# Rotary part once per group of three token tiles, and the work of GpSimd on data in both projections moved to VectorE

## The chip, the cores and the metric

The kernel runs on one core of a Trainium2 chip. The metric is the device time of one execution in microseconds (us); the median of three runs of the kernel before is 2882.1 us (2879.1 to 2884.48). A core has five engines with an instruction queue each: TensorE (PE in the rows, with its weight loads as PEld), VectorE (DVE), ScalarE (ACT), GpSimd (POOL) and SyncE (SP), which issues the DMAs. An engine works its queue in order; a semaphore holds an instruction until what it reads is there.

## The reference

Two layers, each with one input projection of 128 context tokens and 2048 latent tokens (17 tiles of 128), four mixers side by side, an output projection, a residual and a layer norm:

```python
h = x * (1 + scale) + shift
u = h @ p['w_in'] + p['b_in']
...
gq = rms_norm(gq.reshape(B, L, GQA_HEADS, HEAD_DIM), p['q_norm'])     # 4 heads of 64
gk = rms_norm(gk.reshape(B, L, GQA_KV_HEADS, HEAD_DIM), p['k_norm'])  # 2 heads of 64
...
g_out = blocked_attention(axial_rope(gq), ...axial_rope(gk)...)
c_out = conv_mix(c_v, c_glu, ...)   # val * sigmoid(glu), 31 taps along the tokens, LayerNorm, silu, 256x256 product
...
x = layer_norm(DEEPNORM_ALPHA * x + gate * out, p['ln_g'], p['ln_b'])
```

`rms_norm(x, g)` is x / sqrt(mean(x*x) + eps) * g; `axial_rope` turns pairs of a head's columns by angles that depend on the token's place in a 64-wide grid. Context tokens get no rotation. Everything is float32.

## The kernel before

**Precision.** Each factor of a large product is split into a high part (a copy on ScalarE to the engine's reduced float format) and a low part (value minus high part, one subtract). The product is three matmuls: high by high, low by high, high by low (lines 300 to 302). So every operand costs a copy on ScalarE and a subtract; before, most of the subtracts run on GpSimd: `hlo` of the activations (L385, the odd pieces; the even ones on VectorE), `wlo` of the weights (L419), `evl` (L597), `ql` and `ks` of the rotated queries and keys (L722, L732), the convolution's and the pool's operands (L824, L891) and `mlo` of the output projection (L1493).

**Stages.** In each layer phase 1 is the input projection (`_phase1`), phase 2 the grouped-query attention, phase 3 the neighbourhood attention, phase 4 the output projection (`_phase4`). In the profiled execution phase 1 runs from 0 to 727 us in the first layer and from 1490 to 2142 in the second, phase 4 from 1228 to 1490 and from 2640 to 2875.

**Phase 1.** The tokens are taken in two halves, and in each half the column blocks of the projection in a fixed order: three blocks of the convolution, then `gkv` (keys and values), `gq` (queries), and others. `gkv` and `gq` are worked by token tiles: 24 matmuls of 128x256 a tile, into one of five PSUM buffers named `ps_u`. VectorE takes a tile out of PSUM (`qb`, L657, and for values `gve`, L660). So the tile five further on can't begin before that is done.

**What a tile of `gkv` and `gq` sets off.** ScalarE squares it, VectorE sums the squares (L671). For three tiles together the reciprocal root `rs` is made; then for each tile VectorE multiplies by `rs` (L691), GpSimd by the norm's weight (L696), VectorE makes the rotation of the tile in four instructions (L713 to L716), ScalarE makes the high part and GpSimd the low one (`ks` L731 and L732, `qd` and `ql` L720 and L722), and TensorE transposes the tile (L738) between the matmuls of a later tile. Which steps come after how many tiles is given by a list, `later.add(n, step)`.

**Lanes.** After every unit of 24 matmuls a `tick` runs due steps and lets other work on: lane A is the 31-tap convolution of the half on VectorE, one instruction a tap and channel block (L769, 128x1166, or 128x1040 in the second half), one a tick in `gkv` and `gq`. The order in each engine's queue is then settled by the framework's scheduler, from its own estimate of the times.

**Phase 4.** For each token tile the mixers' output `mx` is split (`mhi` L1489 on ScalarE, `mlo` L1493 on GpSimd), multiplied, and VectorE makes the residual and the layer norm in instructions of 128x1024 (L1508, L1515, L1516, L1539, L1540), whose result `y` TensorE transposes (L1557). 

Of the kernel before, what the change touches and what calls it, by code (L numbers as in the profile page):

```python
# [122 lines left out]
class Kern:  # L123
# [248 lines left out]
    def prep_hk(self, l, c, k, x, hi, lo, start=False):  # L372
# [30 lines left out]
    def prep_w(self, l, b, half):  # L403
# [10 lines left out]
        for q in range(4):  # L414
# [4 lines left out]
            nc.gpsimd.tensor_tensor(lo[:, ks, :], w, f32(hi[:, ks, :]), op=ALU.subtract)  # L419
# [15 lines left out]
    def _phase1(self, l):  # L435
# [26 lines left out]
        def tick(ins):  # L462
# [93 lines left out]
    def evac_ch(self, l, name, m, g0, n, p):  # L556
# [26 lines left out]
        else:  # L583
# [13 lines left out]
            nc.gpsimd.tensor_tensor(el[:, :n], e[:, :n], f32(eh[:, :n]), op=ALU.subtract)  # L597
# [81 lines left out]
    def rms(self, l, name, t0, nt, nh, qb, rs):  # L679
# [6 lines left out]

        def s1():
# [6 lines left out]
            g = self.qkn[:, 0 if name == "gq" else 1, :]  # L694
# [7 lines left out]
        def s2(t):  # L702
            tg = t0 + t
            if tg:
                t1 = self.rp.tile([128, 256], F32, tag="t1", name="t1")
                t2 = self.rp.tile([128, 256], F32, tag="t2", name="t2")
                v1 = t1[:, :w].rearrange("p (h d) -> p h d", d=64)
                v2 = t2[:, :w].rearrange("p (h e d) -> p h e d", e=2, d=32)
                qv = q4[:, t]
                qs = qb[:, t, :w].rearrange("p (h e d) -> p h e d", e=2, d=32)  # L710
                cb = rp[:, t, 0, :].unsqueeze(1).to_broadcast([128, nh, 64])
# [32 lines left out]
        for t in range(nt):  # L744
            self.later.add(1 + (t + 1) // 2, lambda t=t: s2(t))
# [981 lines left out]
```

## Time and profile before

| | |
|---|---|
| median of three runs | 2882.1 us |
| profiled execution, device time | 2877.41 us |
| its span, first to last instruction | 2875.5 us |
| mean granted TensorE clock, share of full speed | 0.986 |
| TensorE, VectorE, ScalarE, GpSimd busy | 96%, 68%, 38%, 38% |

The shares are means over stages with different limits: TensorE is the busy one nearly everywhere, so what counts is where it stood still, where it ran at a lower granted clock, and what it waited for then. An engine that is busy less than TensorE can still be full in a short stretch.

### The profile page before, as it was taken

The numbers are of one execution on the slowest core, as the hardware profiler recorded it, in microseconds if no ns is written. First come the engines' busy times: TensorE is split into PE (matmuls) and PEld (weight loads), VectorE is DVE, ScalarE is ACT, GpSimd is POOL, SyncE is SP. The second block draws the span as 40 slices with busy tenths as digits, with TensorE's granted clock in tenths as the row PEclk, the third lists the DMA queues.
The fourth block names the chain that finished last, engine by engine and source line by source line (L and its number), as shares of the span: only waits on it lengthen the run. The fifth ranks groups of instructions, "written<-read, shape, count | busy, mean of one in ns | idle before, by whom it ended". The sixth has DMA issues, their size and how long they took to land. (4 is left out here: it accounts for less than half of the span.)

```text
span 2875.5 us, 45443 instructions
## 1 busy us (share of the span) xinstructions
PE 2773.3 (96%) x16960; PEld 2265.7 (79%) x16960; DVE 1963.2 (68%) x3503; ACT 1080.6 (38%) x1922; POOL 1093.0 (38%) x716
## 2 busy tenths in 40 slices
PE   8999999999999999999999999999999999999998
PEld 6989989999555556887889899999985555578887
DVE  2895247944488886749868952398437888677587
ACT  4233431333344445542222344313424444465210
POOL 4353320411466666014322533213225666720232
PEclk9999999999899999999999999999999999999999
DMA  8676675655451005647755556746555201076343
GB/s 324 206 214 202 196 248 184 211 185 152 96 140 35 21 21 155 166 139 242 234 182 182 171 184 176 239 146 222 154 151 129 67 21 35 8 204 184 132 168 103
DMA packets 330876, 447.79 MB, mean 156 GB/s; under 512 B 54176, under 2 KB 266656, under 8 KB 327840
## 3 DMA queue, kind: packets, MB, share of 16 engines
q1 hardware_dynamic: 330656, 444.89, 51.0%
q8 instruction: 134, 2.20, 0.3%
q14 instruction: 86, 0.70, 0.1%
HBM read 279.39 MB, written 165.39 MB: 155 GB/s over the span
## 5 line engine op out<-in xcount | busy, mean ns | idle before, releaser
L300 PE MATMUL ps_u<-hhi,whi 128*128 128x384 f32 (+1 forms) x1712 | 564.8, 333 | 10.3 <-ACT hhi L383 5.6
L301 PE MATMUL ps_u<-hlo,whi 128*128 128x384 f32 (+1 forms) x1712 | 564.4, 330 | 0.9 <-DVE hlo L385 0.7
L302 PE MATMUL ps_u<-hhi,wlo 128*128 128x384 f32 (+1 forms) x1712 | 562.9, 329 | 0.5 <-POOL wlo L419 0.4
L1053 POOL TENSOR_TENSOR zp<-zp,e 128x1024 f32<-128x1024 f32 x160 | 386.7, 2417 | 217.5 <-ACT e L1035 213.9
L1035 ACT ACTIVATE e<-ps_d 128x1024 f32<-128x1024 f32 x288 | 292.5, 1026 | 361.8 <-PE ps_d L1033 328.9
L769 DVE SCALAR_TENSOR_TENSOR cacc<-cz,small,cacc 128x1166 f32<-128x1166 f32 (+1 forms) x240 | 355.8, 1483 | 3.5
L300 PEld LDWEIGHTS ps_u<-hhi,whi 128*128 128x128 f32 x1712 | 324.0, 190 | 19.5 <-ACT hhi L383 9.4
L301 PEld LDWEIGHTS ps_u<-hlo,whi 128*128 128x128 f32 x1712 | 324.2, 189 | 5.3 <-issue 1.7
L302 PEld LDWEIGHTS ps_u<-hhi,wlo 128*128 128x128 f32 x1712 | 324.0, 189 | 3.2 <-POOL wlo L419 1.4
L956 DVE TENSOR_REDUCE mx<-ps_s 128x1 f32<-128x512 f32 (+1 forms) x374 | 228.5, 631 | 123.3 <-PE ps_s L953 119.3
L1041 PE MATMUL ps_a<-e,gvv 128*64 128x512 f32 x1152 | 280.9, 609 | 0.0
L1493 POOL TENSOR_TENSOR mlo<-mx,mhi 128x512 fp32r<-128x512 f32 x66 | 109.7, 1683 | 407.1 <-ACT mhi L1489 322.6
L300 PE MATMUL ps_u<-whi,hhi 128*128 128x256 f32 x816 | 236.3, 290 | 0.0
L302 PE MATMUL ps_u<-whi,hlo 128*128 128x256 f32 x816 | 235.1, 288 | 0.0
L301 PE MATMUL ps_u<-wlo,hhi 128*128 128x256 f32 x816 | 235.1, 288 | 0.0
L419 POOL TENSOR_TENSOR wlo<-ws,whi 128x512 fp32r<-128x512 f32 x92 | 136.2, 1490 | 211.3 <-ACT whi L418 195.1
L1522 PE MATMUL ps_d<-woh,mhi 128*128 128x512 f32 x512 | 200.3, 391 | 0.0
L1523 PE MATMUL ps_d<-wol,mhi 128*128 128x512 f32 x512 | 200.2, 391 | 0.0
L1524 PE MATMUL ps_d<-woh,mlo 128*128 128x512 f32 x512 | 199.6, 390 | 0.0
L1015 PE MATMUL ps_d<-q,k 128*128 128x512 f32 x576 | 187.9, 409 | 2.3 <-ACT e L1035 1.7
L1033 PE MATMUL ps_d<-q,k 65*128 65x512 f32 x560 | 178.3, 400 | 0.0
L1041 PEld LDWEIGHTS ps_a<-e,gvv 128*64 128x64 f32 x1152 | 71.7, 137 | 127.5 <-issue 125.1
(285 smaller groups left out, 5488.2 us busy)
## 6 DMA issues: line engine op xcount, KB each, us to landing
ws<-in_w_in SPq DMA_DIRECT2D x96, 256.0 KB
mw<-in_w_mod SPq DMA_DIRECT2D x32, 512.0 KB
nq<-s_nq SPq DMA_DIRECT2D x64, 256.0 KB
mx<-s_mix SPq DMA_DIRECT2D x16, 1024.0 KB
s_gate<-ev SPq DMA_DIRECT2D x80, 192.0 KB
s_qh<-qT SPq DMA_DIRECT2D x34, 256.0 KB
x<-in_x SPq DMA_DIRECT2D x17, 512.0 KB
s_xT<-xo SPq DMA_DIRECT2D x17, 512.0 KB
```

The source lines that it names most:

```text
L300: mm(p, ah, bh, start=(k == 0), stop=False)
L301: mm(p, ah, bl, start=False, stop=False)
L302: return mm(p, al, bh, start=False, stop=(k == 7))
L769: nc.vector.scalar_tensor_tensor(acc[:, c, :n], z[:, k:k + n], cw[:, c, k:k + 1], acc[:, c, :n], op0=ALU.mult, op1=ALU.add)
L956: r = nc.vector.tensor_reduce(mx[:, h, i:i + 1], p[:, :n], axis=AX.X, op=ALU.max)
L1015: nc.tensor.matmul(s[:, kv * 512:(kv + 1) * 512], k1[kv][:, j * 128:(j + 1) * 128], q1[:, 2 * kv:2 * kv + 2, :].rearrange("p h t -> p (h t ...
L1035: nc.scalar.activation(e, s, AF.Exp)
L1041: nc.tensor.matmul(acc[kv * 64:(kv + 1) * 64, :], vv[:, j, kv * 64:(kv + 1) * 64], e[:, kv * 512:(kv + 1) * 512], start=(j == 0), stop=(j ...
L1053: nc.gpsimd.tensor_tensor(zp, zp, e, op=ALU.add)
L1522: nc.tensor.matmul(o, hi[:, k, :], woh[:, k, ns], start=(k == 0), stop=False)
L1523: nc.tensor.matmul(o, hi[:, k, :], wol[:, k, ns], start=False, stop=False)
L1524: nc.tensor.matmul(o, lo[:, k, :], woh[:, k, ns], start=False, stop=(k == 7))
```

## The change

Four things. (1) The rotation works on a group of three tiles: the norm's weight is multiplied into the table of cosines and sines (`rp`), once a group, and then five instructions do what 12 on VectorE and three on GpSimd did, beside one multiply by `rs` where there were three. The context tile gets a table row made of the weight and of zero, by GpSimd. (2) The subtracts named above are given to VectorE. (3) `h` (L382, before on VectorE outside the start) is made by ScalarE. (4) The tap lane does no tap or one, alternately, in a tick of `gq`, and the step `s2` of the group's tile t stands t+1 ticks behind, in place of 1+(t+1)//2. The lines of the kernel after are a few lower: L653 is the old L657, L667 the old L671, L694 the old L691, L703 and L706 the old L713 to L716, L727 the old L732, L733 the old L738, L764 the old L769, L415 the old L419.

```diff
-            if start:
-                nc.scalar.activation(h[:, a:b], x[:, a:b], AF.Identity, bias=sh, scale=sc)
-            else:
-                nc.vector.tensor_scalar(h[:, a:b], x[:, a:b], sc, sh, op0=ALU.mult, op1=ALU.add)
+            nc.scalar.activation(h[:, a:b], x[:, a:b], AF.Identity, bias=sh, scale=sc)
...
-        eng = nc.gpsimd if k % 2 or start else nc.vector
-        eng.tensor_tensor(lo[:, k, :n], h[:, :n], f32(hi[:, k, :n]), op=ALU.subtract)
+        nc.vector.tensor_tensor(lo[:, k, :n], h[:, :n], f32(hi[:, k, :n]), op=ALU.subtract)
...
-            nc.gpsimd.tensor_tensor(lo[:, ks, :], w, f32(hi[:, ks, :]), op=ALU.subtract)
+            nc.vector.tensor_tensor(lo[:, ks, :], w, f32(hi[:, ks, :]), op=ALU.subtract)
...
-                for _ in range(1 if name in ("gkv", "gq") else 2):
+                for _ in range({"gkv": 1, "gq": 1 - odd}.get(name, 2)):
...
+        tab = rp[:, l0 - t0:nt].rearrange("p t c d -> p (t c) d")
+        nc.vector.tensor_tensor(tab, tab, g.unsqueeze(1).to_broadcast([128, k, 64]), op=ALU.mult)
+        if t0 == 0:
+            nc.gpsimd.memset(rp[:, 0, 1, :], 0.0)
+            nc.gpsimd.tensor_copy(rp[:, 0, 0, :], g)
...
-            for t in range(nt):
-                nc.vector.tensor_tensor(
-                    q4[:, t], q4[:, t], rs[:, t, :nh].unsqueeze(2).to_broadcast([128, nh, 64]), op=ALU.mult
-                )
-            for t in range(nt):
-                nc.gpsimd.tensor_tensor(
-                    q4[:, t], q4[:, t], g.unsqueeze(1).to_broadcast([128, nh, 64]), op=ALU.mult
-                )
+            nc.vector.tensor_tensor(
+                q4, q4, rs[:, :nt, :nh].unsqueeze(3).to_broadcast([128, nt, nh, 64]), op=ALU.mult
+            )
...
+            for i in range(2):
+                cb = rp[:, :nt, i, :].unsqueeze(2).to_broadcast([128, nt, nh, 64])
+                nc.vector.tensor_tensor(v[i], q4, cb, op=ALU.mult)
+            for f in range(2):
+                nc.vector.tensor_tensor(o[:, :, :, f, :], a[:, :, :, f, :], b[:, :, :, 1 - f, :], op=ALU.add)
...
-                nc.vector.tensor_tensor(v1, qv, cb, op=ALU.mult)
-                nc.vector.tensor_tensor(v2[:, :, :, 0:16], qs[:, :, :, 16:32], sb[:, :, :, 0:16], op=ALU.mult)
-                nc.vector.tensor_tensor(v2[:, :, :, 16:32], qs[:, :, :, 0:16], sb[:, :, :, 16:32], op=ALU.mult)
-                nc.vector.tensor_tensor(qb[:, t, :w], t1[:, :w], t2[:, :w], op=ALU.add)
...
-                nc.gpsimd.tensor_tensor(ql, q4[:, t], f32(qd[:, :, 0, :]), op=ALU.subtract)
+                nc.vector.tensor_tensor(ql, q4[:, t], f32(qd[:, :, 0, :]), op=ALU.subtract)
...
-                nc.gpsimd.tensor_tensor(ks[:, :, 1, :], q4[:, t], f32(ks[:, :, 0, :]), op=ALU.subtract)
+                nc.vector.tensor_tensor(ks[:, :, 1, :], q4[:, t], f32(ks[:, :, 0, :]), op=ALU.subtract)
...
-            self.later.add(1 + (t + 1) // 2, lambda t=t: s2(t))
+            self.later.add(1 + t, lambda t=t: s2(t))
```

The same swap of `nc.gpsimd` for `nc.vector` stands at L597, L824, L891 and L1493. GpSimd's queue goes from 721 instructions to 253, VectorE's from 3505 to 3639, ScalarE's from 1780 to 1876; TensorE's and SyncE's keep theirs. The scheduler then orders the queues anew.

TensorE in the second layer, the first place where a transpose of keys stands among the matmuls of a `gkv` tile (`ps_u`: the tile's PSUM buffer, `ps_d`: the transpose's, `idr`: the identity). Before, it is in the sixth tile of the block:

```order
L301 MATMUL ps_u_15794<-wlo_15423,hhi_14793 128x256
L302 MATMUL ps_u_15794<-whi_15422,hlo_14794 128x256
L300 MATMUL ps_u_15794<-whi_15422,hhi_14793 128x256
L738 MATMUL ps_d_15786<-idr_63,ks_15676 128x128 x2
L301 MATMUL ps_u_15794<-wlo_15423,hhi_14793 128x256
L302 MATMUL ps_u_15794<-whi_15422,hlo_14794 128x256
L300 MATMUL ps_u_15858<-whi_15422,hhi_14959 128x256
```

After, the first two stand together in the ninth tile:

```order
L302 MATMUL ps_u_15768<-whi_15262,hlo_14800 128x256
L300 MATMUL ps_u_15768<-whi_15262,hhi_14799 128x256
L301 MATMUL ps_u_15768<-wlo_15263,hhi_14799 128x256
L733 MATMUL ps_d_15618<-idr_63,ks_15520 128x128 x2
L733 MATMUL ps_d_15660<-idr_63,ks_15579 128x128 x2
L302 MATMUL ps_u_15768<-whi_15262,hlo_14800 128x256
L300 MATMUL ps_u_15768<-whi_15262,hhi_14799 128x256
```

The transposes moved back by three tiles, while the matmuls around them are the same.

VectorE in the same layer, in the block of queries of the first half (`cacc` is a tap of the convolution, `t` the products of the rotation, `rp` its table). Before, the rotation goes tile by tile, between taps:

```order
L713 TENSOR_TENSOR t_16339<-qb,rp 128x256
L714 TENSOR_TENSOR t_16340<-qb,rp 128x8x16
L715 TENSOR_TENSOR t_16340<-qb,rp 128x8x16
L769 SCALAR_TENSOR_TENSOR cacc<-cz,small,cacc 128x1166
L713 TENSOR_TENSOR t_16381<-qb,rp 128x256
L714 TENSOR_TENSOR t_16382<-qb,rp 128x8x16
L715 TENSOR_TENSOR t_16382<-qb,rp 128x8x16
L716 TENSOR_TENSOR qb<-t_16339,t_16340 128x256
L657 TENSOR_TENSOR qb<-ps_u,btok 128x256 x3
L769 SCALAR_TENSOR_TENSOR cacc<-cz,small,cacc 128x1166
```

After, a group of three tiles goes through in a few wider instructions, and the low parts of weights and keys stand between them:

```order
L706 TENSOR_TENSOR qb<-t_15812,t_15813 128x3x4x16 x2
L694 TENSOR_TENSOR qb<-qb,rs 128x768
L764 SCALAR_TENSOR_TENSOR cacc<-cz,small,cacc 128x1166
L686 TENSOR_TENSOR rp<-rp,qkn 128x384
L727 TENSOR_TENSOR ks<-qb,ks 128x2x64 x2
L703 TENSOR_TENSOR t_15945<-qb,rp 128x768
L703 TENSOR_TENSOR t_15946<-qb,rp 128x768
L764 SCALAR_TENSOR_TENSOR cacc<-cz,small,cacc 128x1166
L727 TENSOR_TENSOR ks<-qb,ks 128x2x64
L706 TENSOR_TENSOR qb<-t_15945,t_15946 128x24x16 x2
L764 SCALAR_TENSOR_TENSOR cacc<-cz,small,cacc 128x1166
L653 TENSOR_TENSOR qb<-ps_u,btok 128x256 x3
```

Where three instructions for a tile and one tap alternated, two wide products and two wide sums now stand, with `L727`, which was GpSimd's, between them.

## Rows read from the trace of the kernel before

**Rows 1.** The page's first part: busy time, share of the span, instructions.

```profile
PE 2773.3 (96%) x16960; PEld 2265.7 (79%) x16960; DVE 1963.2 (68%) x3503; ACT 1080.6 (38%) x1922; POOL 1093.0 (38%) x716
```

**Rows 2.** TensorE's waits: us in total, times, longest us.

```profile
PE ps_d L738 <- POOL ks L732: 12.0, 8, 3.5
PE ps_d L738 <- ACT qd L720: 9.0, 7, 3.2
...
PE ps_s L1557 <- DVE y L1540: 3.7, 5, 1.9
...
PE ps_d L795 <- DVE cacc L769: 2.4, 1, 2.4
```

**Rows 3.** Busy time by stretch; last columns: clock, DMA share, GB/s.

```profile
132.00:172.00 40.00, 34.71 (x281) 32.53 (x282) 36.49 (x84) 12.28 (x39) 19.05 (x25) 0.87 0.59 182
205.00:212.00 7.00, 5.97 (x36) 5.06 (x35) 7.00 (x16) 2.71 (x5) 3.10 (x3) 1.00 0.70 217
1576.00:1608.00 32.00, 26.29 (x192) 25.55 (x192) 30.80 (x65) 9.11 (x25) 17.48 (x19) 0.89 0.58 177
1636.00:1672.00 36.00, 29.09 (x167) 27.93 (x166) 35.66 (x60) 14.74 (x29) 20.26 (x19) 0.95 0.66 210
```

**Rows 4.** TensorE's timeline at such a wait, start and duration in us.

```profile
131.21 0.28 PE L300 MATMUL ps_u<-whi,hhi 128*128 128x256 f32 x1
134.75 0.50 PE L738 MATMUL ps_d<-idr,ks 128*128 128x128 f32 x2 [3.26 <-POOL ks L732]
```

**Rows 5.** The same view by stretch, second layer, convolution to the queries' end.

```profile
1562.00:1642.00 80.00, 71.62 (x535) 69.89 (x534) 77.64 (x135) 23.89 (x58) 40.96 (x38) 0.96 0.56 175
sum 122.00, PE 113.62 PEld 111.89 DVE 118.78 ACT 34.27 POOL 50.11; mean PE 56.81 PEld 55.94 DVE 59.39 ACT 17.14 POOL 25.05
```

**Rows 6.** VectorE's costliest lines from 1520 to 1642 us.

```profile
L769 DVE SCALAR_TENSOR_TENSOR cacc<-cz,small,cacc 128x1166 f32<-128x1166 f32 x49 | 80.6, 1646 | 0.9
L691 DVE TENSOR_TENSOR qb<-qb,rs 128x128 f32<-128x128 f32 (+1 forms) x15 | 7.0, 519 | 0.0
L715 DVE TENSOR_TENSOR t<-qb,rp 128x64 f32<-128x64 f32 (+1 forms) x12 | 6.1, 512 | 0.0
...
L713 DVE TENSOR_TENSOR t<-qb,rp 128x128 f32<-128x128 f32 (+1 forms) x12 | 5.5, 459 | 0.8 <-POOL qb L696 0.6
...
L716 DVE TENSOR_TENSOR qb<-t,t 128x128 f32<-128x128 f32 (+1 forms) x11 | 3.6, 335 | 0.0
```

**Rows 7.** VectorE's timeline in the second layer's queries.

```profile
1636.09 0.94 DVE L713 TENSOR_TENSOR t<-qb,rp 128x256 f32<-128x256 f32 x1 [0.63 <-POOL qb L696]
...
1638.44 2.46 DVE L769 SCALAR_TENSOR_TENSOR cacc<-cz,small,cacc 128x1166 f32<-128x1166 f32 x1
1640.83 0.41 DVE L713 TENSOR_TENSOR t<-qb,rp 128x256 f32<-128x256 f32 x1
...
1641.90 1.07 DVE L657 TENSOR_TENSOR qb<-ps_u,btok 128x256 f32<-128x256 f32 x3
```

**Rows 8.** GpSimd's timeline in the same stretch.

```profile
1634.18 3.45 POOL L696 TENSOR_TENSOR qb<-qb,qkn 128x256 f32<-128x256 f32 x3
...
1638.33 1.34 POOL L419 TENSOR_TENSOR wlo<-ws,whi 128x512 fp32r<-128x512 f32 x1
```

**Rows 9.** VectorE's timeline in the first layer, a tap at its shortest.

```profile
119.90 1.42 DVE L769 SCALAR_TENSOR_TENSOR cacc<-cz,small,cacc 128x1166 f32<-128x1166 f32 x1
121.24 0.27 DVE L671 TENSOR_REDUCE rs<-sq 128x2 f32<-128x128 f32 x1
```

**Rows 10.** All of line 1493: duration in ns, least, median, most.

```profile
L1493 POOL TENSOR_TENSOR mlo<-mx,mhi x66: 1267/1313/2357, 1231.2 to 2847.1; 128x512 fp32r<-128x512 f32 x66
...
L1493 DVE TENSOR_TENSOR mlo<-mx,mhi x2: 691/692/693, 1229.8 to 2641.4; 128x512 fp32r<-128x512 f32 x2
```

**Rows 11.** Who waited for line 382: us in total, times.

```profile
  ACT hhi L383: 86.1, 53
```

**Rows 12.** Busy time in phase 4 of the first layer.

```profile
1300.00:1368.00 68.00, 64.70 (x312) 53.20 (x311) 63.29 (x77) 20.84 (x43) 30.40 (x20) 1.00 0.75 244
```

More of the change, by code (lines that the diff above doesn't have):

```diff
@@ L596, in evac_ch @@
             el = self.e2.tile([128, 384], F32R, tag="evl", name="evl")
-            nc.gpsimd.tensor_tensor(el[:, :n], e[:, :n], f32(eh[:, :n]), op=ALU.subtract)
+            nc.vector.tensor_tensor(el[:, :n], e[:, :n], f32(eh[:, :n]), op=ALU.subtract)
             for hh in range(2):
@@ L685, in rms @@
         nc.sync.dma_start(rp[:, l0 - t0:nt], A["rope"][:, l0 - 1:t0 + nt - 1])
+        g = self.qkn[:, 0 if name == "gq" else 1, :]
+        k = 2 * (t0 + nt - l0)
+        tab = rp[:, l0 - t0:nt].rearrange("p t c d -> p (t c) d")
[3 more added lines that the diff above has]
+            nc.gpsimd.tensor_copy(rp[:, 0, 0, :], g)
         def s1():
@@ L689, in s1 @@
             nc.vector.reciprocal(rs[:, :nt, :nh], rs[:, :nt, :nh])
-            for t in range(nt):
-                nc.vector.tensor_tensor(
-                    q4[:, t], q4[:, t], rs[:, t, :nh].unsqueeze(2).to_broadcast([128, nh, 64]), op=ALU.mult
-                )
-            g = self.qkn[:, 0 if name == "gq" else 1, :]
-            for t in range(nt):
-                nc.gpsimd.tensor_tensor(
-                    q4[:, t], q4[:, t], g.unsqueeze(1).to_broadcast([128, nh, 64]), op=ALU.mult
-                )
+            nc.vector.tensor_tensor(
+                q4, q4, rs[:, :nt, :nh].unsqueeze(3).to_broadcast([128, nt, nh, 64]), op=ALU.mult
+            )
+            t1 = self.rp.tile([128, 3, 256], F32, tag="t1", name="t1", bufs=1)
+            t2 = self.rp.tile([128, 3, 256], F32, tag="t2", name="t2", bufs=1)
+            v = [x[:, :nt, :w].rearrange("p t (h d) -> p t h d", d=64) for x in (t1, t2)]
+            for i in range(2):
+                cb = rp[:, :nt, i, :].unsqueeze(2).to_broadcast([128, nt, nh, 64])
+                nc.vector.tensor_tensor(v[i], q4, cb, op=ALU.mult)
+            o, a, b = [x[:, :nt, :w].rearrange("p t (h f d) -> p t h f d", f=2, d=16) for x in (qb, t1, t2)]
+            for f in range(2):
+                nc.vector.tensor_tensor(o[:, :, :, f, :], a[:, :, :, f, :], b[:, :, :, 1 - f, :], op=ALU.add)
             if t0 == 0 and name == "gkv":
@@ L823, in conv_post @@
             nc.scalar.activation(shi[:, c, :n], s32[:, :n], AF.Copy)
-            nc.gpsimd.tensor_tensor(slo[:, c, :n], s32[:, :n], f32(shi[:, c, :n]), op=ALU.subtract)
+            nc.vector.tensor_tensor(slo[:, c, :n], s32[:, :n], f32(shi[:, c, :n]), op=ALU.subtract)
             yield
@@ L890, in pool_jobs @@
             nc.scalar.activation(yhi[:, :n], y, AF.Copy)
-            nc.gpsimd.tensor_tensor(ylo[:, :n], y, f32(yhi[:, :n]), op=ALU.subtract)
+            nc.vector.tensor_tensor(ylo[:, :n], y, f32(yhi[:, :n]), op=ALU.subtract)
             if i + 1 < len(items):
@@ L1491, in prep @@
                     self.midact = getattr(r, "ins", r)
-                eng = nc.vector if t == 0 and k.start == 0 else nc.gpsimd
-                eng.tensor_tensor(lo[:, k], m[:, k, ms], f32(hi[:, k]), op=ALU.subtract)
+                nc.vector.tensor_tensor(lo[:, k], m[:, k, ms], f32(hi[:, k]), op=ALU.subtract)
             hl[t] = (hi, lo)
@@ L1658, in layouts @@
         rope[:, 0, o + 16:o + 32] = co
-        rope[:, 1, o:o + 16] = -si
-        rope[:, 1, o + 16:o + 32] = si
+        rope[:, 1, o:o + 16] = si
+        rope[:, 1, o + 16:o + 32] = -si
     m["rope"] = c(rope.reshape(L // 128, 128, 2, 64).transpose(1, 0, 2, 3))
```

9 lines of the change are left out of this document (removed).

## The prediction, made before the changed kernel was run

> **What bounds the kernel now.** I read the busy shares of the page first, then TensorE's waits, then the busy time of every engine by stretch, and last the two queues that release the waits, line by line and in order of time.
>
> TensorE is busy 2773.3 of the 2875.5 us of the span [rows 1], so 102 us of idle time, and what a lower granted clock costs on top, are all that a change which leaves the matmuls alone can win. The list of waits shows the largest group: the transposes of rotated keys and queries, L738, waited 12.0 us in 8 cases for the low part of keys on GpSimd and 9.0 us in 8 cases for the high part of queries on ScalarE [rows 2]. A longest case shows how it looks: the matmul at 131.21 is followed by nothing until 134.75, a wait of 3.26 us [rows 4]. The instruction waiting is small, but it stands in the queue among the matmuls of a later tile, so all of TensorE waits.
>
> The view by stretch says what this costs in all [rows 3]. The four stretches are the blocks of keys and queries of the first half of the tokens, two in each layer. In their 115.0 us TensorE is busy 96.06 by the four rows together, so 18.94 us are idle. The granted clock is 0.87, 0.89 and 0.95 in three of them, against 1.00 in the fourth: 0.13 x 40 + 0.11 x 32 + 0.05 x 36 = 10.5 us more. Together 29.5 us stand to be had. In the same stretches VectorE is busy 109.95 us, 96%. So the engine that ends these waits is VectorE, though the list names GpSimd and ScalarE: both work on what VectorE hands them, and they are far from full there.
>
> **Why VectorE is full there, and what the change makes of it.** From 1520 to 1642 us, the convolution's last block up to the sixteenth tile of the second layer, VectorE is busy 118.78 of 122 us [rows 5]. 49 taps take 80.6 us of it, 1.646 each, and the multiply by the root and the rotation take 62 instructions of 28.3 us (7.0 + 6.1, and L714 the same 6.1, + 5.5 + 3.6) [rows 6]. But a tap takes 1.42 us at its shortest, and the next instruction starts 1.34 after it: an instruction is covered by its successor for 0.08 us [rows 9]. What stretches them stands beside them in time: at 1636.09 the product of the rotation takes 0.94 us while GpSimd does three multiplies by the weight, and at 1640.83 the same takes 0.41 with GpSimd's queue empty; the tap at 1638.44 takes 2.46 beside a weight subtract of GpSimd [rows 7, 8].
>
> The rule behind it is in the Trainium skill, "SBUF — State Buffer", section "Who interferes with whom": the two engines share a port pair, and a VectorE instruction that needs it and a GpSimd one lock each other out. The rows agree in direction; the tap lost 1.04 us, less than the 1.34 of the GpSimd instruction beside it, so a plain sum of lock times would overstate the gain.
>
> I now count VectorE's queue up to the evacuation of the sixteenth tile in the order after, and price each instruction start to start, its shortest duration less 0.08:
>
> - 46 taps (three fewer, by the lane that skips every other tick of the queries) at 1.34: 61.6.
> - 14 weight subtracts of 128x512 that were GpSimd's, at the 0.69 that VectorE took for this shape in the output projection [rows 10], less 0.08: 8.5.
> - 9 `ks` of 128x128 at 0.27 [rows 9] and 3 `ql` of 128x256 at 0.41 [rows 7]: 2.7.
> - Rotation and root, 25 instructions in place of 62. The shapes are wider than any of before: 0.41 for 256 columns and 0.69 for 512 give 0.28 for 256 more, so 0.55 for 384, 0.97 for 768, 0.34 for 192. Four table products at 0.55, 3 x 0.55 + 2 x 0.97 for the root, 6 x 0.55 + 2 x 0.97 for the products, 6 x 0.34 + 2 x 0.55 for the sums are 14.2, less 25 x 0.08: 12.2. If a strided sum costs by columns as the uncontended tap does (1.42 for 1166), nothing changes; if each cost as in the stretched rows it would be some 20.
> - The other 49 instructions: before they took 118.8 - (80.6 - 3.9) - (28.3 - 5.0) = 18.8 us; at the least 49 x 0.20 [rows 9] = 9.8. I take 14.
>
> The sum is 99 us against 118.8, with the last item's ends 95 to 104. So VectorE comes to the sixteenth tile about 17 us sooner (some of its 3 us of idle stay), at 1625 and not 1642. TensorE lost 8.4 us idle and 0.04 x 80 = 3.2 by the clock from 1562 to 1642 [rows 5], and without these it would come to the same point at 1630. VectorE is then 5 us ahead of TensorE where it was behind.
>
> In the first layer the count gives 40 taps, 16 weight subtracts and the same rotation, and only some 6 us are won, while TensorE has 10.5 us to win from 132 to 172 [rows 3]; so there I keep part of the loss.
>
> **The sum.** Against the profiled execution, 2877.4 us (span 2875.5):
>
> - The waits of the transposes and their clock: -29.5.
> - Waits that stay or are new: +10. In the order after, a transpose of keys stands three tiles later, which at 24 matmuls of 0.12 us (131.21 is one of a row of such) is some 8 us more room against a longest wait of 3.5 [rows 2]. But a tile's keys now come only after the whole group of three. I keep 5 us for the PSUM buffers in the first layer, by the 4.5 us that VectorE stays behind there, and 5 us for 4 of the 16 waits at their mean of 1.3. The ends are 0 and the whole 21.
> - The clock in two of these: +3.5 (the stretch from 1636 on lost 1.8 with one wait of that size [rows 3]); ends 0 and 10.5.
> - The wait of L795 for the last tap [rows 2]: -2.4. With the taps shorter it goes; at worst it stays.
> - Output projection: `mlo` and the weights go to VectorE, which was busy 63.29 of 68 us in its fullest part [rows 12]. `mlo` costs 0.69 there against a median of 1.31 on GpSimd [rows 10]. The 66 `mlo` lie in some 500 us of the two output projections, so 9 in those 68 us, 6.2 us more on VectorE, where 4.7 are free; but the pieces of `h` for the next layer leave it, and what runs beside GpSimd, which the queries' rows show up to twice as long, gets shorter (GpSimd is busy 30.40 us there). I take these as even, so the wait of L1557 for `y`, 3.7 us, mostly goes: -2.5 (ends -3.7 and +4, if VectorE fills up and nothing gets shorter).
> - `h` on ScalarE, 96 instructions: ScalarE had already waited 86.1 us for `h` in its queue [rows 11], and is busy 12.28 of 40 us in the full stretch [rows 3], so this is hidden, except at the start and where a half begins, where nothing else is ready: +1.5 (0 to 8, for 8 pieces of 0.5 at two places).
> - The rest that leaves GpSimd (`evl`, the convolution's and pool's operands) lies beside matmuls and has slack: 0 (-2 to 2). TensorE's and SyncE's instructions keep their number.
>
> -29.5 + 10 + 3.5 - 2.4 - 2.5 + 1.5 = -19.4, so 2858.0 in the state of the profile. That execution was 4.7 us below the median of the three runs, 2882.1; so the forecast there is 2862.7, rounded 2863.
>
> **Rivals.**
>
> *The waits only move.* The late step isn't VectorE's load but the round trip VectorE, ScalarE, VectorE, TensorE. A step of a group of three comes later for its first tile, and a `ks` in VectorE's queue stands behind taps of 1.4 us each, up to two. For it: the list names ScalarE in 8 of the 16 waits [rows 2]. Against: VectorE's 96% and the later place of the transposes. Then 29.5 us are lost as before in another line, and the time is that of before, 2878 to 2886.
>
> *VectorE becomes the bound.* If the stretch of the taps is not GpSimd's doing (DMAs run at 0.56 to 0.70 share too [rows 3, 5]), 46 taps stay at 1.57 start to start, 72 us; the weight subtracts then cost up to what GpSimd's took, 1.34 less 0.08, 14 x 1.26 = 17.6; with 2.7, 12.2 and 18.8 the sum is 123.3, 4.5 more than before. TensorE is then held at the PSUM buffers, from the twenty-first tile on, in place of the transposes: 4.5 us in each layer, half as much again by the clock (10.5 to 18.94 in rows 3), 13.5 in all, and 1.5 at the start; won are only the two small terms, 2.4 and 2.5: 2882.1 + 15 - 4.9 = 2892. It decides from taps of 1.6 us mean on. Against it: 0.41 and 0.94 us for the same instruction [rows 7].
>
> The Trainium skill's "Perfetto Trace Analysis", section "Optimizing Scalar/DVE Operations", says that when VectorE is saturated, offloading some of its work to another engine may make sense, and adds that between VectorE and GpSimd it might not help, for the shared port. Its first half speaks for this rival, its second against; the rows with 0.94 and 0.41 bear out the second.
>
> *A larger gain.* All 21 us of L738 with their clock go and the start costs nothing: 2882.1 - 29.5 - 4.9 = 2848.
>
> **How the numbers follow.** Forecast 0.60, larger gain 0.06, waits only move 0.18, VectorE the bound 0.16. About 0.2% (5.8 us) is what a measurement of this kernel can tell from no change: faster is below 2876, slower above 2888. The forecast's own range is 2850 to 2876. Faster 0.66, within 0.2% 0.18, slower 0.16. For 8 in 10 the range takes the forecast, half the larger gain and the case in which the waits move: 2846 to 2888.
>
> **What would show it.** Right: taps of a mean near 1.45 from the convolution's block to the queries' end; VectorE's busy share there clearly under 97%; L733 (the old L738) with less than 10 us of waits; a clock of 0.95 or more in the stretches of rows 3; `mlo` at 0.7 on VectorE. Wrong: taps at 1.6 or more, or waits of `ps_u` for L653 or L656 (the evacuations) as long as those of L738 now; transposes waiting 15 us or more for `ks` and `qd`; a wait of TensorE at the start that grows by more than 4 us.

## The result and the profile after

The kernel after takes 2847.5 us, the median of four runs (2840.28 to 2852.52), against 2882.0 before (four runs). The ratio is 0.9878, 95% interval 0.9860 to 0.9896: 1.2% faster. The forecast was 2863 with a range of 2846 to 2888; the time lies at the lower end, by the case called the larger gain (2848); that it lies just there is chance, as the terms below show. The profiled execution of after took 2852.5 us (span 2850.7), 5.0 above its median, where that of before stood 4.7 below: the two traces differ by 24.8 us and the medians by 34.5. The traces show where the time went, not all of it.

The first part of the page after [rows 1]. GpSimd's busy time is halved, VectorE's is nearly the same, though it does 134 instructions more:

```profile
PE 2765.4 (97%) x16960; PEld 2269.4 (80%) x16960; DVE 1970.4 (69%) x3637; ACT 1132.4 (40%) x2018; POOL 550.7 (19%) x248
```

TensorE's waits after [rows 2]; L733 is the old L738, L653 the evacuation, L1551 the old L1557:

```profile
PE ps_s L1551 <- DVE y L1534: 5.7, 3, 3.4
PE ps_d L1551 <- DVE y L1534: 5.3, 1, 5.3
...
PE ps_u L300 <- DVE qb L653: 2.9, 3, 2.3
...
PE ps_d L733 <- DVE ks L727: 1.9, 1, 1.9
...
PE ps_d L733 <- ACT qd L715: 1.2, 1, 1.2
```

The 21.0 us of the transposes are 3.1. The wait for `y` in the output projection grew from 3.7 to 11.0. Busy time by stretch after, columns as in rows 3, two of the stretches shown there and those beside them (the second layer's work comes 9 to 21 us sooner):

```profile
132.00:172.00 40.00, 39.41 (x361) 37.59 (x359) 36.47 (x75) 11.24 (x36) 1.44 (x2) 1.00 0.61 196
172.00:212.00 40.00, 38.24 (x254) 36.83 (x255) 37.71 (x70) 18.13 (x37) 0.00 (x0) 0.96 0.71 230
212.00:255.00 43.00, 43.00 (x320) 42.59 (x319) 32.43 (x58) 15.33 (x29) 0.00 (x0) 1.00 0.69 226
...
1561.00:1593.00 32.00, 32.00 (x274) 32.00 (x273) 29.64 (x65) 11.24 (x31) 0.51 (x2) 1.00 0.65 208
1593.00:1621.00 28.00, 24.59 (x164) 24.05 (x163) 28.00 (x45) 9.64 (x23) 0.00 (x0) 0.88 0.47 140
1621.00:1652.00 31.00, 31.00 (x192) 30.86 (x191) 26.63 (x49) 15.37 (x30) 0.00 (x0) 1.00 0.71 230
```

And of before, the stretch behind those of rows 3 in the first layer, which the prediction had not looked at:

```profile
212.00:266.00 54.00, 48.95 (x343) 48.05 (x342) 34.10 (x69) 20.07 (x34) 17.98 (x14) 0.98 0.66 209
```

The key and query blocks lost 29.5 us before. Now the rows from 132 to 212 and from 1561 to 1652 lose 5.8 us idle (0.59 + 1.76 + 3.41) and 5.0 by the clock (0.04 x 40 + 0.12 x 28). What is left stands in two places, and in the larger, from 1593 to 1621, VectorE is busy all the time.

VectorE's lines from 1520 to 1642 us [rows 6]: the taps are back at 1.425, the rotation and the root are L703, L694, L706 and L686:

```profile
L764 DVE SCALAR_TENSOR_TENSOR cacc<-cz,small,cacc 128x1166 f32<-128x1166 f32 x49 | 69.8, 1425 | 0.5
L415 DVE TENSOR_TENSOR wlo<-ws,whi 128x512 fp32r<-128x512 f32 x17 | 11.5, 686 | 2.6 <-ACT whi L414 2.5
L703 DVE TENSOR_TENSOR t<-qb,rp 128x384 f32<-128x384 f32 (+1 forms) x12 | 8.5, 751 | 0.0
...
L694 DVE TENSOR_TENSOR qb<-qb,rs 128x384 f32<-128x384 f32 (+1 forms) x6 | 4.5, 753 | 0.0
L706 DVE TENSOR_TENSOR qb<-t,t 128x192 f32<-128x192 f32 (+1 forms) x10 | 3.9, 432 | 0.0
L686 DVE TENSOR_TENSOR rp<-rp,qkn 128x384 f32<-128x384 f32 (+1 forms) x5 | 2.6, 527 | 1.4 <-DMA rp<-in_rope 1.4
```

The three query tiles whose evacuation ended the block before at 1641.90 [rows 7] come out of PSUM here:

```profile
1617.79 1.07 DVE L653 TENSOR_TENSOR qb<-ps_u,btok 128x256 f32<-128x256 f32 x3
```

Since TensorE's queue has the same matmuls in every kernel here, the start of its n-th matmul can be set against that in the trace of before. The differences, taken from stage to stage, say what each stage gave or cost (us; one trace each). Behind the ratio of the median times with its interval stands how far the traced execution lay from its kernel's median; that of before lay 4.7 below:

```
                         start  keys/queries  rest of  to output   output proj.  keys/queries  rest to  ratio to before         traced less
                                1st half, l.1 layer 1  projection  and switch    1st half, l.2 the end                           median
after                     +3.3     -14.0       -3.4      -0.3        +8.8          -14.6        -4.6    0.9878 (0.9860-0.9896)   +5.0
e1 group only             +0.1     -11.4       -1.4      +0.8        +6.2           -6.4        +0.1    0.9914 (0.9894-0.9935)   +5.0
e2 engines only           +0.7     -12.2      +11.5      +0.3        +8.9          -12.4        +7.2    0.9955 (0.9940-0.9969)   +8.4
e3 late transposes        +0.1      +0.9       +0.5      -2.3        +4.3           +9.2        +1.3    1.0043 (1.0027-1.0059)   -6.4
e4 GpSimd repeats         +4.9      -2.2       -2.6      -0.9        +8.7           -2.9        +2.3    0.9987 (0.9976-0.9999)   +2.4
e5 mlo on GpSimd          +4.1     -11.3       -1.7      -1.7        +0.6          -11.7        -1.7    0.9886 (0.9870-0.9902)   -0.2
e6 h on VectorE           +1.2     -13.0       -4.1      +5.4        +5.6          -16.4        -2.5    0.9875 (0.9857-0.9893)   +2.3
e7 weights on GpSimd      +4.3     -10.3       +0.4      -3.3        +2.5           -7.2        -1.2    0.9920 (0.9902-0.9939)   -1.4
e8 switch weights         +3.0     -15.8       +0.1      -1.0        +6.0          -14.3        -0.3    0.9878 (0.9861-0.9896)   +1.5
e9 tap at every tick      +2.8     -12.0       +2.0      -3.4       +10.6          -18.4        -2.3    0.9911 (0.9892-0.9931)   -5.3
e10 taps thinner          +2.5     -13.3       +3.9      -0.2        +9.5          -14.2        +5.2    0.9922 (0.9904-0.9940)   +6.0
e11 mlo and h             -0.6     -12.8       +3.8      -0.2       +10.7          -11.8        -2.0    0.9882 (0.9861-0.9904)  +13.7
e12 GpSimd reads along    +4.1      -1.1       -4.2      -2.5        +9.2          -10.4        +0.7    0.9921 (0.9900-0.9941)   +6.6
```

The stages end before the matmuls number 340, 1700, 4900, 7600, 9010 and 10030 (64.1, 266.0, 719.3, 1233.7, 1494.3 and 1668.1 us in before). After, e5 and e8 have the same program up to the output projection, so the spread of their first three columns (1.1, 4.5 and 3.5 us) is what one trace can't tell.

### The profile page after: what moved, and what is told of

It reads as the page before. It is cut to its first block, busy times and chain, and to the rows that moved or that the text cites. A ratio compares the mean times of both kernels' runs of the same rounds, so it can differ in the third digit from the quotient of the medians.

```text
span 2850.7 us, 44895 instructions
## 1 busy us (share of the span) xinstructions
PE 2765.4 (97%) x16960; PEld 2269.4 (80%) x16960; DVE 1970.4 (69%) x3637; ACT 1132.4 (40%) x2018; POOL 550.7 (19%) x248
## 4 chain that ended last, share of the span: by engine, by line
PE 71%; DMA 12%; DVE 11%; ACT 2%; SPq 2%; issue 2%; POOL 0%; DVEq 0%; ACTq 0%; POOLq 0%
PE ps_u L300 9%; PE ps_u L301 8%; PE ps_u L302 8%; PE ps_a L1036 8%; PE ps_d L1010 5%; PE ps_d L1028 4%; PE ps_d L1517 3%; PE ps_d L1516 3%; PE ps_d L1518 3%; PE ps_a L1295 3%; PE ps_s L948 3%; DVE cacc L764 2%; DMA ws<-in_w_in 2%; PE ps_z L948 2%; PE ps_s L1280 2%
## 5 line engine op out<-in xcount | busy, mean ns | idle before, releaser
L764 DVE SCALAR_TENSOR_TENSOR cacc<-cz,small,cacc 128x1166 f32<-128x1166 f32 (+1 forms) x240 | 325.9, 1358 | 2.8
L1044 DVE TENSOR_TENSOR zd<-zd,e 128x1024 f32<-128x1024 f32 x80 | 140.2, 1753 | 45.0 <-ACT e L1030 45.0
L300 PEld LDWEIGHTS ps_u<-whi,hhi 128*128 128x128 f32 x816 | 156.5, 192 | 5.3 <-DVE qb L653 3.5
```

Of the source, the lines that this page charges most:

```text
L300: mm(p, ah, bh, start=(k == 0), stop=False)
L764: nc.vector.scalar_tensor_tensor(acc[:, c, :n], z[:, k:k + n], cw[:, c, k:k + 1], acc[:, c, :n], op0=ALU.mult, op1=ALU.add)
```

## The experiments

The runs were made on several chips, each against before on the same chip; before was 2882.0 to 2889.1 us there, so kernels are compared by their ratios. 0.001 is 2.9 us.

**e1, grouping without the engines.** From the kernel after:

```diff
-        nc.vector.tensor_tensor(... op=ALU.subtract)   # each of the eight subtracts
+        nc.gpsimd.tensor_tensor(... op=ALU.subtract)   # hlo and mlo split as before; h on VectorE
```

> The kernel after, with every subtract given back to GpSimd and h to VectorE as before; left of the change are the rotation by groups, the weight folded into the table, the lane that skips every other tick and the later steps. Theory A (VectorE's queue in the key and query blocks of the first half is what held TensorE; it got shorter both by fewer instructions and by less GpSimd work beside it): 37 rotation instructions fewer take some 11 us out of a block, the taps stay near 1.6 us, so about half of the gain: 2862 to 2870, with L733 still waiting 6 to 12 us. Theory B (the gain is the later place of the transposes in TensorE's queue; here they stand nearly where they stood before, a tile or two earlier than in the kernel after): 2872 to 2882. Theory C (only GpSimd's work beside VectorE mattered): 2875 to 2882, taps at 1.6.

Measured: 2860.3, ratio 0.9914. TensorE's waits for the transposes (there L737), and the taps over the whole kernel in before, after and e1:

```profile
PE ps_d L737 <- POOL ks L731: 8.4, 6, 2.6
...
PE ps_d L737 <- ACT qd L719: 3.5, 2, 2.6
```

```profile
L769 DVE SCALAR_TENSOR_TENSOR cacc<-cz,small,cacc 128x1166 f32<-128x1166 f32 (+1 forms) x240 | 355.8, 1483 | 3.5
L764 DVE SCALAR_TENSOR_TENSOR cacc<-cz,small,cacc 128x1166 f32<-128x1166 f32 (+1 forms) x240 | 325.9, 1358 | 2.8
L768 DVE SCALAR_TENSOR_TENSOR cacc<-cz,small,cacc 128x1166 f32<-128x1166 f32 (+1 forms) x240 | 352.4, 1468 | 3.5
```

As theory A said: the taps stay stretched, the waits halve (11.9 us), and more than half of the gain is there, 25 of 35 us, a little more than expected. C, as it was put, falls by this run: the grouping gains with GpSimd's subtracts all in place. But the grouping also rids GpSimd of three multiplies a group, and the run doesn't part that from the fewer instructions on VectorE.

**e2, engines without grouping.** From the kernel before, all subtracts and the multiply by the weight go to VectorE, and `h` to ScalarE:

```diff
-                nc.gpsimd.tensor_tensor(
+                nc.vector.tensor_tensor(
                     q4[:, t], q4[:, t], g.unsqueeze(1).to_broadcast([128, nh, 64]), op=ALU.mult
                 )
...
```

> The kernel before, with all subtracts and the multiply by the norm weight on VectorE and h on ScalarE, but the rotation tile by tile, the lane and the steps as before. Theory A: taps near 1.42, but VectorE gets 14 weight subtracts, the multiplies and the ks, and keeps 62 rotation instructions; by start-to-start prices some 113 us of queue against 119 before and 99 after, so a third of the gain: 2865 to 2874. Theory C (GpSimd beside VectorE is all): 2847 to 2855. Rival of the prediction (VectorE becomes the bound): above 2885. Theory B: the transposes stand one to four tiles later here too, so 2848 to 2860.

Measured: 2872.8, ratio 0.9955, in the range of A. Its trace has taps as short as after:

```profile
L765 DVE SCALAR_TENSOR_TENSOR cacc<-cz,small,cacc 128x1166 f32<-128x1166 f32 (+1 forms) x240 | 326.4, 1360 | 2.7
```

The table shows what the expectation had not: in the first half's key and query blocks it gains nearly what after gains (12.2 and 12.4 us), and loses it in the rest of each layer (+11.5, +7.2). Part of that loss may be the traced execution, which lies 8.4 us above its median. In the first layer, 7.3 us of it are three waits from 640 to 770 us for the products `jo` and the maxima `mx` that VectorE makes there, 4.2 us the longest. That it is the moved subtracts beside the small rotation instructions which make VectorE late is likely, but not shown.

**e3, late transposes alone.** From the kernel before; the transposes are held back to the tiles where they stand in after:

```diff
-                self.later.add(2, lambda: s3(...))
+                self.later.add(6, lambda: s3(...))
...
+            with self.tc.issue_after(self.lastu):   # the last matmul of the unit before
                 for i in range(n):
                     nc.tensor.transpose(...)
```

> The kernel before, with one thing changed: the transposes of keys and queries are held back in TensorE's queue, to the tiles where they stand in the kernel after (28 to 35 of the first layer's units, 184 to 192 of the second's). VectorE's and GpSimd's work is that of before. Theory B (place): most of the gain, 2850 to 2862, L738 waiting under 5 us, VectorE as late as before at the sixteenth tile but TensorE not waiting for it. Theory A: VectorE is as full as before, the lag goes on growing behind the later transposes, and the waits come back at the PSUM buffers or at the queries: 2868 to 2882.

Measured: 2898.1, ratio 1.0043, slower than either theory said, but for the reason of A:

```profile
PE ps_d L740 <- ACT qd L721: 10.0, 7, 3.3
PE ps_d L740 <- POOL ks L733: 8.7, 4, 3.4
...
PE ps_u L300 <- DVE gve L661: 7.4, 2, 3.8
...
PE ps_u L300 <- DVE qb L658: 5.3, 2, 2.7
```

The transposes wait 18.7 us, as before 21.0, and TensorE now waits 12.7 us at the PSUM buffers besides. The later place did not help the transposes while their producer was as full as before: B falls. The loss beyond A's range was not taken apart; the other queues were ordered anew too.

**e4, GpSimd repeats the weight subtracts.** From the kernel after:

```diff
             nc.vector.tensor_tensor(lo[:, ks, :], w, f32(hi[:, ks, :]), op=ALU.subtract)
+            nc.gpsimd.tensor_tensor(lo[:, ks, :], w, f32(hi[:, ks, :]), op=ALU.subtract)
```

> The kernel after, where GpSimd makes each weight subtract a second time behind VectorE's (same values, into the same tile); 92 instructions of 128x512 more on GpSimd, nothing less on VectorE. Theory A with the shared access as the cause: taps beside them go from 1.42 to 2 us and over, the mean of a tap from 1.36 to about 1.45, VectorE's queue in a block grows by some 10 us, and 5 to 10 us of the gain go: 2853 to 2858. Theory B: 2844 to 2850, since the transposes keep their places. If the stretch of the taps is not GpSimd's doing: taps stay at 1.36.

Measured: 2883.0, ratio 0.9987, nearly all of the gain gone, three times what A allowed. VectorE's and then GpSimd's timeline show how the two meet:

```profile
1601.70 2.47 DVE L765 SCALAR_TENSOR_TENSOR cacc<-cz,small,cacc 128x1166 f32<-128x1166 f32 x1
...
1608.74 1.43 DVE L765 SCALAR_TENSOR_TENSOR cacc<-cz,small,cacc 128x1166 f32<-128x1166 f32 x1
...
1610.39 2.36 DVE L765 SCALAR_TENSOR_TENSOR cacc<-cz,small,cacc 128x1166 f32<-128x1166 f32 x1
```

```profile
1601.52 1.41 POOL L416 TENSOR_TENSOR wlo<-ws,whi 128x512 fp32r<-128x512 f32 x1 [1.58 <-DVE wlo L415]
...
1608.90 2.62 POOL L416 TENSOR_TENSOR wlo<-ws,whi 128x512 fp32r<-128x512 f32 x1 [2.76 <-DVE wlo L415]
```

Of a tap and a weight subtract, whoever begins second stands until the first is done. GpSimd's subtract begun at 1601.52 ends at 1602.93, and the tap begun at 1601.70 ends 1.24 us after that. The tap begun at 1608.74 ends at 1610.17, and GpSimd's begun at 1608.90 ends 1.35 after that, its full 1.34 [rows 8]; the next tap, begun at 1610.39, ends 1.23 after that again. But the taps do not make up all of this run's loss, 31 us by the ratios:

```profile
L765 DVE SCALAR_TENSOR_TENSOR cacc<-cz,small,cacc 128x1166 f32<-128x1166 f32 (+1 forms) x240 | 344.6, 1436 | 2.9
```

They are 18.7 us longer than after in all (344.6 against 325.9). The weights' tiles also come free later, behind GpSimd, and VectorE, with `wlo` in its queue, waits for `whi` up to 4.7 us; a transpose waited 8.2 us for `ks` at once (11.4 in 3 cases). So this run mixes two costs, and e7 and e12 were made to part them.

**e5, mlo back on GpSimd.** From the kernel after:

```diff
-                nc.vector.tensor_tensor(lo[:, k], m[:, k, ms], f32(hi[:, k]), op=ALU.subtract)
+                eng = nc.vector if t == 0 and k.start == 0 else nc.gpsimd
+                eng.tensor_tensor(lo[:, k], m[:, k, ms], f32(hi[:, k]), op=ALU.subtract)
```

> The kernel after, with only mlo of the output projection back on GpSimd. The trace after shows TensorE waiting 11.0 us for y in the first layer's output projection (before 3.7). Theory D (the mlo in VectorE's queue make y late): the waits of L1551 fall to 4 us or less, 2838 to 2843. Theory E (y is late because ScalarE, and behind it VectorE, stand at the head of their queues for the weights of the second layer, which come by DMA): the waits stay at 8 to 12, and the taps' like stretch comes back on the 1024-wide instructions: 2847 to 2853.

Measured: 2854.5, ratio 0.9886, not told apart from after. The wait for `y` is 5.1 us, and the stage of the output projection is 8 us shorter than after in the traces, as D says; the time did not follow. e11 below, with the same edit, waits 10.1 us for `y`.

**e6, h back on VectorE.** From the kernel after, the removed branch of L382 is put back.

> The kernel after, with only h made on VectorE as before. The prediction had +1.5 us for h on ScalarE, with 0 and 8 as ends; the trace after lies 3.4 us behind that of before after 64 us. If h on ScalarE is what costs there: 2842 to 2846, and the first 64 us as long as before. If it is the clock of the start and the DMAs, which differ from run to run: 2846 to 2851.

Measured: 2851.1, ratio 0.9875. The start is 2 us shorter in the table (of the nine kernels with `h` on ScalarE eight show +2.5 to +4.9, e2 +0.7; the four without show -0.6 to +1.2), but in the time there is no difference.

**e7, weight subtracts back on GpSimd.** From the kernel after:

```diff
-            nc.vector.tensor_tensor(lo[:, ks, :], w, f32(hi[:, ks, :]), op=ALU.subtract)
+            nc.gpsimd.tensor_tensor(lo[:, ks, :], w, f32(hi[:, ks, :]), op=ALU.subtract)
```

> The kernel after, with only the weight subtracts back on GpSimd: against the run in which GpSimd repeats them, VectorE is rid of its own 92 subtracts of 0.69 us (start to start 56 us in all, 8.5 of it in a block of keys and queries). Theory A: GpSimd's instructions cost VectorE what they took there (taps of 1.44 mean, as in that run), less 8.5 us a block: 2860 to 2872. If a shared access costs VectorE no more than the subtract itself: 2845 to 2852.

Measured: 2863.8, ratio 0.9920, 12 us slower than after by the ratios, as A says, though VectorE is rid of 92 instructions:

```profile
PE ps_d L733 <- DVE ks L727: 8.5, 6, 1.9
...
PE ps_d L733 <- ACT qd L715: 5.9, 4, 3.1
```

```profile
L764 DVE SCALAR_TENSOR_TENSOR cacc<-cz,small,cacc 128x1166 f32<-128x1166 f32 (+1 forms) x240 | 347.9, 1450 | 3.3
```

Taps of 1.45 and waits of 14.4 us are back. The gain goes in the first half's key and query blocks: 3.7 and 7.4 us less than after in the table, the first within the spread of one trace.

**e8, weights at the layer switch on GpSimd.** From the kernel after; ScalarE's copy and VectorE's subtract of the first block's weights, loaded during the output projection, go to GpSimd. It was made for a place in the trace of after, ScalarE's timeline, where the copy of a weight waits for its DMA and the root that VectorE's layer norm needs (L1528) stands behind it:

```profile
1354.16 0.63 ACT L414 ACTIVATE whi<-ws 128x512 fp32r<-128x512 f32 x1 [5.99 <-DMA ws<-in_w_in]
1354.70 0.28 ACT L1528 ACTIVATE mv<-mv,eps_ln 128x1 f32<-128x1 f32 x1
```

```diff
-            nc.scalar.activation(hi[:, ks, :], w, AF.Copy)
-            nc.vector.tensor_tensor(lo[:, ks, :], w, f32(hi[:, ks, :]), op=ALU.subtract)
+            if l and b == 0:
+                nc.gpsimd.tensor_copy(hi[:, ks, :], w)
+            else:
+                nc.scalar.activation(hi[:, ks, :], w, AF.Copy)
+            (nc.gpsimd if l and b == 0 else nc.vector).tensor_tensor(lo[:, ks, :], w, f32(hi[:, ks, :]), op=ALU.subtract)
```

> The kernel after, where the high and low parts of the weights loaded during the first layer's output projection (the first block of the second layer, four pieces) are made by GpSimd, which has nothing else to do there. Theory E: ScalarE and VectorE no longer stand behind a DMA; the waits of L1551 in the first layer fall from 11.0 to 5 or less and 5 to 7 us go: 2839 to 2844. Theory D: no change in these waits, 2846 to 2851.

Measured: 2853.4, ratio 0.9878. The waits (there L1554) fall only from 11.0 to 9.0, and the longest stays:

```profile
PE ps_d L1554 <- DVE y L1537: 5.4, 1, 5.4
```

The place for which this run was made gives 2.1 us (`ps_s` waits 3.6 us in all there, 5.7 after). The longest wait of all lies elsewhere, at the last token tile of the projection. In the trace of after:

```profile
1472.20 0.21 DVE L1527 BATCH_NORM_AGGREGATE mv<-st 128x2 f32<-128x12 f32 x1
1473.26 1.28 ACT L1528 ACT_TABLE_LOAD   x1
1474.55 0.29 ACT L1528 ACTIVATE mv<-mv,eps_ln 128x1 f32<-128x1 f32 x1
1476.95 0.69 DVE L415 TENSOR_TENSOR wlo<-ws,whi 128x512 fp32r<-128x512 f32 x1 [1.91 <-ACT whi L414]
1477.56 1.41 DVE L1534 SCALAR_TENSOR_TENSOR y<-y,mv,lnb 128x512 f32<-128x512 f32 x2
1478.36 1.97 PE L1551 MATMUL ps_d<-small,y 128*128 128x128 f32 x8 [5.30 <-DVE y L1534]
```

The layer norm's variance is there at 1472.41. The root on ScalarE stands behind an activation of the next layer and behind a load of its table, 1.28 us; then VectorE stands 1.91 us at a weight subtract whose `whi` isn't there; so `y` begins 5.36 us after L1527. In e5 neither stands between, and it is 1.77. e8 has the same order as after, with 2.03 us at such a subtract, since it moved other weights. So E, an engine that stands at the head of its queue for a weight, is not refuted: it is part of the longest wait.

**e9 and e10, the tap lane.** From the kernel after, one number each:

```diff
-                for _ in range({"gkv": 1, "gq": 1 - odd}.get(name, 2)):
+                for _ in range({"gkv": 1, "gq": 1}.get(name, 2)):          # e9
+                for _ in range({"gkv": 1 - odd, "gq": 1 - odd}.get(name, 2)):   # e10
```

> The kernel after, with only the tap lane of the query block as before (a tap at every tick). Theory A: six taps more stand before the last query tiles of a half, 8 us of VectorE's queue at 1.34 each; VectorE has little room in that block (74.8 of 80 us busy), so 3 to 8 us are lost: 2850 to 2856. If the lane doesn't matter: 2845 to 2851.

> The kernel after, with the tap lane thinned in the key block too (no tap or one, alternately, in keys and queries). Theory A: if VectorE's queue in these blocks still holds TensorE, 3 to 6 us are won (2841 to 2846), and the taps that are put off must not end later than the half's last convolution product. If the queue is no longer the bound there: 2846 to 2851, or slower by the taps put off, with a wait for cacc.

Measured: 0.9911 (0.9892 to 0.9931) and 0.9922 (0.9904 to 0.9940), both slower than after by 10 and 13 us. But neither run tests what it was made for. In the traces the instructions of TensorE and of VectorE stand in the order of after through all blocks of keys and queries (in e10 but for one evacuation), taps included: whatever the lane offered, the scheduler set them in the same places. Accordingly these stages give as much as after, within the spread (-12.0 and -18.4, -13.3 and -14.2). What differs is the order of the convolution's and the pool's work behind these blocks, and in the rest of the first layer the traces lose 2.0 and 3.9 us where after gains 3.4. So what a tap more or fewer there is worth stays open, and a change of order elsewhere can take 10 us. In e10 the attention waits for the convolution's last product:

```profile
PE ps_d L948 <- DVE jo L831: 7.1, 4, 3.4
```

**e11, mlo on GpSimd and h on VectorE together.** The edits of e5 and e6 in one kernel.

> The kernel after, with mlo of the output projection back on GpSimd and h back on VectorE: the two parts of the change that the runs so far show as costs of their own places (the first layer's output projection 8 us longer than before, the first 64 us 3 us longer). If these add up: 2838 to 2844. If what is won there is given back behind, as with mlo alone: 2846 to 2852.

Measured: 0.9882 (0.9861 to 0.9904), no better than after: the two don't add up to a gain. In its trace, which lies 13.7 us above the median, the wait for `y` is 10.1 us in six cases and the stage of the output projection 10.7 us longer than before, with `mlo` on GpSimd as in e5.

**e12, GpSimd reads along.** From the kernel after:

```diff
+            for j in range(2 if b else 0):
+                scr = self.rp.tile([128, 128], F32, tag="scr", name="scr", bufs=1)
+                nc.gpsimd.tensor_tensor(scr, w[:, j, :128], f32(hi[:, q * 2 + j, :128]), op=ALU.subtract)
```

> The kernel after, where GpSimd also subtracts, for each weight piece but those of the first block, two parts of 128x128 into a scratch tile that nobody reads; 176 instructions more on GpSimd, and no engine waits for them but for the release of the loaded piece. TensorE's and VectorE's queues are the same as in the kernel after up to and past the first layer's key and query blocks of the first half. It parts what GpSimd's presence costs from what a longer chain through GpSimd costs (the run with repeated subtracts had both). Theory A with the shared access: taps beside these go to 2 us and over, the mean tap to 1.40 or more, and some 5 to 15 us are lost: 2855 to 2865 by the pace of this kernel. If the loss with the repeated subtracts was the chain alone: taps at 1.36 and 2846 to 2851.

Measured: 0.9921 (0.9900 to 0.9941), 12 us slower than after, as A says of the time; not so the taps:

```profile
L767 DVE SCALAR_TENSOR_TENSOR cacc<-cz,small,cacc 128x1166 f32<-128x1166 f32 (+1 forms) x240 | 331.1, 1380 | 2.8
```

```profile
L418 POOL TENSOR_TENSOR scr<-ws,whi x176: 452/792/7536, 47.8 to 1811.9; 128x128 f32<-128x128 f32 x176
```

A mean of 1.380 is less than the 1.40 asked for: beside GpSimd instructions this short it is GpSimd that stands, in one case 7.5 us for one of 0.45. That holds the loaded weight piece, and ScalarE waits for the next one. The transposes (there L736) wait 14.7 us again:

```profile
PE ps_d L736 <- ACT qd L718: 8.6, 3, 6.4
PE ps_d L736 <- DVE ks L730: 6.1, 4, 2.9
```

So extra work on GpSimd does cost TensorE time: the queues of TensorE, VectorE and ScalarE have the order of after until 326 us, and still the first layer's blocks of keys and queries give 1.1 us, where three traces of after's order gave 11.3 to 15.8. The taps are 5.2 us longer in the whole kernel (331.1 against 325.9), so they are not all of the 12; how much the late weights are stays open.

## Why the prediction was right, step by step

**The bound.** Right. That VectorE's queue was behind the waits is shown by e3 (their place changed: no gain) and by e1 and e2, which shorten the queue in two different ways and both win. e12 shows it from the other side: the queues in the same order, more work on GpSimd, and the waits are back.

**The sum of VectorE's queue.** Right. Taps at 1.42, weights at 0.69, `ks` at 0.28, 384 columns at 0.55 and 768 at 0.95 were priced 1.42, 0.69, 0.27, 0.55 and 0.97. The sixteenth to eighteenth tiles come 24.1 us earlier (1617.79 for 1641.90). The blocks of the second layer begin 8.6 us sooner (the matmul that starts at 1560.0 before), so the queue won 15.5, forecast 17. The 46 taps before them, three fewer than before, were counted rightly but not for the reason given, the lane: e9, with the lane of before, has VectorE's instructions there in the same order.

**Waits that stay, +10 and +3.5.** Within their ends, 5.8 and 5.0, together 10.8 for 13.5, though not where I put them: 3.4 of the first stand in the second layer, and in the first layer one evacuation was waited for, 2.3 us.

**The sum, -19.4.** In the traces it is -24.8. For the key and query blocks and what lies beside them the terms were -29.5 + 13.5 - 2.4 = -18.4, and the two stages of the table show -28.6. Of the 10.2 between, 2.7 are the waits that stay. 3.7 are the last term, which was too small: TensorE lost 5.05 us idle and 1.1 by the clock from 212 to 266 before, where VectorE's late taps held the convolution's product, and nothing after; I had counted one wait of 2.4 there. Some 3 us more were won before the second layer's blocks (TensorE is 5.6 us ahead at the matmul that starts at 1494.3 before, 8.6 at that of 1560.0). The rest of the layers, which I put at nothing, gave 8.3 us (3.4, 0.3 and 4.6); which waits these were was not taken apart. The start and the output projection, below, took 12.1 of it back (3.3 and 8.8), where I had them at -1.0. So the sum came near by misses of both signs: 10.2 and 8.3 us more won than forecast, 13.1 more lost. And 9.7 of the 34.5 us between the medians are the two traces' distances from theirs.

**Output projection, -2.5.** Wrong in sign: the wait for `y` grew by 7.3 us to 11.0. The term went by VectorE's busy time, and of that it was right: in a like stretch (314 matmuls against 312) VectorE is busy 56.48 of 68 us, before 63.29 [rows 12], and `mlo` took 0.683 us as priced.

```profile
1286.00:1354.00 68.00, 65.72 (x314) 54.42 (x313) 56.48 (x75) 26.06 (x55) 1.25 (x1) 1.00 0.70 224
```

What it left out is the order in which the queues reach the layer norm. 5.3 of the 11.0 us are the one wait at the last token tile, shown at e8, and no `mlo` stands in it. It is 4.6 to 5.5 us long in the kernels with `mlo` on VectorE (2.8 in e7, where no weight subtract stands there) and at most 0.2 in before, e1, e3, e5 and e11, where `mlo` is on GpSimd. So the place of `mlo` decides it, by the order that the scheduler then gives to the queues, and not by `mlo`'s own time. The length of the stage doesn't follow from it: with `mlo` on GpSimd it is 0.6 us longer than before in e5, but 10.7 in e11. What sets the rest, and what takes back e5's 8 us, stays open.

**h on ScalarE, +1.5.** +3.3 in the trace of after, 2 more than with `h` on VectorE (e6), and 0.9875 against 0.9878 in the times: within the ends.

**The rivals.** "The waits only move" falls with 3.1 us of L733. "VectorE becomes the bound" rested on taps that stay at 1.6 or weights that cost as on GpSimd; e2 shows where it has a point: with the engines moved and the rotation not grouped, the rest of a layer loses up to 11.5 us, in a trace that lies 8.4 above its median. From before, the grouping with its lane and steps brought 25 us by the ratios and the move alone 13; after either, the other brought 10 and 22.

**The lock.** The prediction said that a tap lost less than the whole GpSimd instruction beside it, so that a sum of locks overstates. The rows of e4 bear this out and say why: the second to begin waits only from its own start until the first has ended, and one that begins first loses nothing. The tap at 1601.70 lost 1.05 beside a GpSimd instruction of 1.41. The rule is in the Trainium skill, "SBUF — State Buffer", section "Who interferes with whom": whoever issues first has the shared pair for its whole instruction, and the other is blocked. These rows agree to 0.2 us (after the wait a tap needs 1.23 or 1.24 more, where it takes 1.42 undisturbed).

## What to carry to other kernels

When a wait names an engine that is a third full, look for the engine that feeds it, and count that one's queue instruction by instruction, from starts, at undisturbed durations. Work that is taken from GpSimd can make the kernel faster although VectorE does more (13 us here), and does so better where fewer and wider instructions make room for it (35 us for both). Holding the waiting instruction back in its own queue gained nothing while its producer was full. And where a scheduler orders the queues, look in the trace whether an edit changed the order that it was meant to change: two edits of the tap lane left the taps where they were.

## What was not expected of the hardware

A GpSimd instruction of 128x128 that takes 0.45 us at its shortest took 7.5 in one case beside VectorE (e12, from 217.00 us; the next longest took 2.7): VectorE went through 12 whole instructions in that time, one behind the other, while the taps grew by 0.02 us in the mean. And traces with the same order of instructions differ by 5.6 us after the first 266 (after, e5 and e8 are 10.7, 7.2 and 12.8 us ahead of before there), so a gain of one stage read from a single trace is no finer than that.
